# Attention logits of two heads as three half-height products side by side, with undoubled keys and a bias of key sums alone

## The chip, the core and the metric

The kernel runs on one core of one Trainium2 chip. The core has a matrix engine (TensorE, PE in the profile; its weight loads are the row PEld), three engines for elementwise work (VectorE or DVE, ScalarE or ACT, GpSimd or POOL) and SyncE (SP), which here only issues transfers. Matmuls write PSUM, eight banks of 128 partitions by 512 words; GpSimd doesn't read PSUM. The metric is the device time of one execution in microseconds (us), the median of several runs; lower is better.

## The reference

Two layers over 512 tokens of width 1024. Layer 0 is sparse attention: an indexer of 8 heads of width 64 scores every key, each query keeps its best keys, and 16 query heads in 4 groups attend to them. Layer 1 is a "forgetting" attention of 16 heads with a causal mask. Both are followed by an MLP with squared ReLU. What matters here is the logits of each:

```python
idx_logits = einsum('bqhd,bsd->bqhs', qib, ki)           # indexer, d = 64
score = einsum('bqhs,bqh->bqs', relu(idx_logits), wib)   # best keys by this score
logits = einsum('bqngd,bqknd->bqngk', qg, k_sel) * scale # attention A, then softmax

log_f = log_sigmoid(f_logit + b_f)                       # attention B: forget gates
cum = cumsum(log_f)
logits = einsum('bqhd,bshd->bhqs', qb, k) * scale
decay = cum[t, h] - cum[s, h]
logits = where(causal, logits + decay, -inf)             # then softmax
```

Everything is in float32. A softmax over the keys s doesn't change when a number that depends on the query t alone is added to its row.

## The kernel before

**Precision.** A float32 matmul is made of matmuls in fp32r, a reduced format. `split` (line 499) makes a high part (ACT writes the rounded copy) and a low part (DVE subtracts it from the source). A full product is then three matmuls, `mm3` (line 534): high by high, high by low, low by high.

**Logits.** A head has width 64, half of the array's 128 rows. Before, the two halves of the rows are used together for one head. `unpair` (line 681) writes for each of two heads a stationary tile with the high part of the query in 64 rows and its low part in the other 64: two ACT operations and two DVE operations, each on 64 partitions. The keys stand twice, in both halves of the rows, once as high and once as low parts. Two matmuls of 128 rows then give all four products of high and low parts:

```python
for i in range(2):
    PE.matmul(b[:, :n], q[:, 128 * t:128 * t + 128], ks[e][:, i, :n], start=i == 0, stop=i == 1)
```

This form stands in three places: `scores` (line 742, the indexer, 8 heads, query blocks 1 to 3), attention A (lines 848 to 905, 4 key heads of 4 query heads, query blocks 0 to 3) and `attn` (line 1433, attention B, 8 pairs of heads, query blocks 0 to 3). A query block is 128 queries; block t sees n = 128(t + 1) keys, so the matmuls have 128, 256, 384 or 512 columns.

In A and in the indexer the keys are doubled when they are transposed (`dup_T`). In B, `kproj` (line 1400) computes the keys of two heads in one bank (24 matmuls) and then writes four tiles' worth from it: four ACT copies and four DVE subtractions, each on 64 partitions by 512.

**Bias of B.** `bias` (line 1421) makes for each head and each query block a tile of cum[t] - cum[s] on GpSimd, with -1e30 above the diagonal: it fetches the row of cum of a head to all 128 partitions from DRAM (`cd`), and per block runs one tensor_scalar (with the query's own sums, `cq`, as a scalar per partition) and one affine_select on the last 128 columns. `cq` comes from four transposes of `cum` on TensorE. A DVE reduction adds a tile to the logits in the bank and takes the row's minimum of the negated sum; ACT then computes the exponentials, GpSimd scales by the reciprocal sum, TensorE transposes, and the products with the values follow.

**Forget gates.** `fb` (line 1322, 16 matmuls with 48 columns) gives the gate logits; a chain of small DVE operations on 16 partitions (lines 1367 to 1389) gives `cum`, after the value projection in the program's order.

**Order of the work.** The program is recorded and then planned: `Recorder.schedule` (line 244) runs a list schedule over the five engines with estimated costs (`cost`, line 210; a matmul of n columns is max(n/2400 + 0.0133, 0.109) us, whatever its rows). The priority of an operation is the place of the program on TensorE's clock at which it stands, or earlier if its successors need it. A tile is taken only when a slot is free: the logits of A and B may hold three of the eight PSUM banks (`"lg": 3`), the transposes four and the value products one; the indexer's banks have no such limit. The planned order is then emitted; each engine executes its instructions in that order.

**Weights.** Weight tiles are split too. Where a stage's number stands in `far`, the low part is made by ACT (a negated copy) and an accumulating transfer issued by GpSimd, not by DVE.

Line 423 of the profile is the helper that emits every operation, so groups are read by their tiles' names: `lg` and `ix` are banks of logits, `qs`, `qo`, `qst` split queries, `kdup`, `kd`, `kid` doubled keys, `bt` bias tiles, `pT` transposes, `pv` value products, `kp`, `qp` key and query projections, `gc` small transposes of gains.

Of the kernel before, what the change touches and what calls it, by code (L numbers as in the profile page):

```python
# [15 lines left out]
T = 512  # L16
# [4 lines left out]
BIG = 3e38  # L21


class View:
# [35 lines left out]
    def row(self, r):  # L60

        ids = np.broadcast_to(self.ids[:1], (2,) + self.ids.shape[1:])
        return View(self.t, ids, self.chain + [("f", lambda ap: bass.AP(
            tensor=ap.tensor, offset=ap[r:r + 1].offset, ap=[[0, 128], [1, ap.shape[1]]]))])

# [60 lines left out]
class Recorder:  # L126
# [22 lines left out]
    def add(self, eng, fn, a, k):  # L149
# [3 lines left out]
        outs = [k["out"]] if "out" in k else [a[0]]  # L153
        ins = [x for x in list(a[0 if "out" in k else 1:]) + [v for q, v in k.items() if q not in ("out", "accum_out")]
               if isinstance(x, View)]
# [3 lines left out]
        if fn == "matmul" and not k.get("start"):  # L159
            ins = ins + outs  # L160
# [10 lines left out]
        if fn == "matmul" and k.get("start"):  # L171
            for p in set(outs[0].t.last.values()):
                op.preds[p] = 1
# [238 lines left out]
    def emit(self, order):  # L412
        def real(x):
            if not isinstance(x, View):
                return x
            t = x.t
            if t.real is None:
                t.real = t.store.real.tile(list(t.shape), t.dt, tag="%s%d" % (t.store.tag, t.at[0]), name=t.name)
            return x.real()
        for o in order:  # L420
            a = [real(x) for x in o.a]
            k = {q: real(v) for q, v in o.k.items()}
            getattr(self.engs[o.eng], o.fn)(*a, **k)  # L423
# [11 lines left out]
    "pace": 1.0, "pvb": (4,), "rcb": True, "bord": (0, 1, 2, 3),  # L435
# [3 lines left out]
def body(ctx, tc, a, out):  # L439
# [241 lines left out]
    def unpair(dst, b, scale):  # L681

        up, dn = slice(0, 64), slice(64, 128)
        if CFG["swap"]:
            hi, lo = scr([128, 512], "nh", F32R), scr([128, 512], "nl", F32R)
            b = b.flat() if len(b.shape) > 2 else b
            split(hi, lo, b, scale=scale)
            d = dst if len(dst.shape) == 3 else View(dst.t, dst.ids.reshape(dst.ids.shape[0], 2, -1),
                                                     dst.chain + [("r", "p e a b -> p e (a b)", {})])
            SP.dma_start(f32(d)[up, 0], f32(hi)[up])  # L690
            SP.dma_start(f32(d)[dn, 0], f32(lo)[up])
            SP.dma_start(f32(d)[dn, 1], f32(hi)[dn])
            SP.dma_start(f32(d)[up, 1], f32(lo)[dn])
            return
        S.activation(dst[up, 0], b[up], AF.Copy, scale=scale)
        S.activation(dst[dn, 1], b[dn], AF.Copy, scale=scale)
        V.scalar_tensor_tensor(dst[dn, 0], b[up], scale, f32(dst[up, 0]), op0=OP.mult, op1=OP.subtract)
        V.scalar_tensor_tensor(dst[up, 1], b[dn], scale, f32(dst[dn, 1]), op0=OP.mult, op1=OP.subtract)
# [149 lines left out]
    for t in range(NT):  # L848
# [3 lines left out]
        for kv in range(4):  # L852
# [3 lines left out]
            for h in range(4):  # L856
                b = bank([128, 512], "lg")
                for p in range(2):
                    PE.matmul(b[:, :n], qs[t][kv // 2][:, h % 2, 2 * (kv % 2) + h // 2, :], kd[kv][:, p, :n],
                              start=p == 0, stop=p == 1)  # L860
# [437 lines left out]
    def qstack(p, b):  # L1298
        unpair(qo[p], b, 0.125)
# [11 lines left out]
    for p in range(4, 8):  # L1311
        b = bank([128, T], "qp")
        featprod(xq, wS(wq, 128 * p), b)
        qstack(p, b)

# [7 lines left out]
    for k in range(8):  # L1323
        for i in range(2):
            PE.matmul(fb[0:48], wf[:, k, :], xk[i][k // 2][:, k % 2, :], start=k + i == 0, stop=k + i == 8)

# [40 lines left out]
    z, f2 = scr([16, T], "z"), scr([16, T], "f2")  # L1367
    S.copy(f2, fb[32:48])
    V.scalar_tensor_tensor(z, fb[0:16], bfc, f2, op0=OP.add, op1=OP.add)
    e = scr([16, T], "e")  # L1370
    V.tensor_scalar(e, z, -1.0, None, op0=OP.mult)
    V.tensor_tensor(e, z, e, op=OP.min)
    S.activation(e, e, AF.Exp)
    V.tensor_scalar(z, z, 0.0, None, op0=OP.min)
    s = scr([16, T], "s")
    V.tensor_scalar(s, e, 2.0, None, op0=OP.add)
    V.reciprocal(s, s)
    V.tensor_tensor(s, s, e, op=OP.mult)
    w2 = scr([16, T], "w2")
    V.tensor_tensor(w2, s, s, op=OP.mult)  # L1380
    V.tensor_scalar(e, w2, 2.0 / 17, 2.0 / 15, op0=OP.mult, op1=OP.add)
    for c in (13, 11, 9, 7, 5, 3, 1):
        V.tensor_tensor(e, e, w2, op=OP.mult)
        V.tensor_scalar(e, e, 2.0 / c, None, op0=OP.add)
    V.tensor_tensor(e, e, s, op=OP.mult)
    V.tensor_tensor(z, z, e, op=OP.subtract)
    cum, zrow = scr([16, T], "cum"), scr([16, T], "zrow")
    V.memset(zrow, 0.0)
    V.tensor_tensor_scan(cum, z, zrow, 0.0, op0=OP.add, op1=OP.add)
    cd = rec.tile(p_dr["cd"], [16, T], F32, "cd")  # L1390
    SP.dma_start(cd, cum)
    cq = const([128, NT, 16], "cq")
    cb = bank([128, NT, 16], "cb")
    for t in range(NT):
        PE.transpose(cb[:, t, :], cum[:, 128 * t:128 * t + 128], ident[0:16, 0:16])
    S.copy(cq, cb)

    lows("k")

    def kproj(p):  # L1400
# [3 lines left out]
        ks = [htile([128, 2, T], "kdup", F32R) for _ in range(2)]  # L1404
        if CFG["dup"]:

            kn = htile([128, 2, T], "kn", F32R)
            split(kn[:, 0, :], kn[:, 1, :], b)
            for e in range(2):
                for o in range(2):  # L1410
                    SP.dma_start(f32(ks[e])[64 * o:64 * o + 64], f32(kn)[64 * e:64 * e + 64])
            return ks
        for e in range(2):
            r, o = slice(64 * e, 64 * e + 64), slice(64 - 64 * e, 128 - 64 * e)
            S.copy(ks[e][r, 0, :], b[r])
            S.copy(ks[e][o, 0, :], b[r])
            V.tensor_tensor(ks[e][r, 1, :], b[r], f32(ks[e][r, 0, :]), op=OP.subtract)
            V.tensor_tensor(ks[e][o, 1, :], b[r], f32(ks[e][r, 0, :]), op=OP.subtract)
        return ks

    def bias(p):
        bt = [rec.tile(p_bt, [128, 2, 128 * (t + 1)], F32, "bt") for t in range(NT)]
        for e in range(2):
            ck = scr([128, T], "ck")
            SP.dma_start(ck, cd.row(2 * p + e))
            for t in range(NT):
                n = 128 * (t + 1)
                G.tensor_scalar(bt[t][:, e, :], ck[:, :n], -1.0, cq[:, t, 2 * p + e:2 * p + e + 1], op0=OP.mult, op1=OP.add)
                dg = bt[t][:, e, n - 128:n]
                G.affine_select(dg, dg, pattern=[[-1, 128]], compare_op=OP.is_ge, fill=NEG, base=0, channel_multiplier=1)  # L1430
        return [[x[:, e, :] for x in bt] for e in range(2)]

    def attn(p, ks, bts):
        pts = {}
        for e in range(2):
            q = qo[p][:, e, :]
            b0, b1, b2 = [bank([128, T], "pT") for _ in range(3)]
            rcs = small(4, "rc") if CFG["rcb"] else None
            sts = small(4, "st") if CFG["rcb"] else None
            ls = {}  # L1440
            l01 = scr([128, 384], "l")
            for t in CFG["bord"]:
                n = 128 * (t + 1)
                b = bank([128, 512], "lg")
                for i in range(2):
                    PE.matmul(b[:, :n], q[:, 128 * t:128 * t + 128], ks[e][:, i, :n], start=i == 0, stop=i == 1)
                l, mn = scr([128, n], "l") if t > 1 else l01[:, 128 * t:128 * t + n], small(1, "mn")
                st = sts[:, t:t + 1] if CFG["rcb"] else small(1, "st")
                V.tensor_tensor_reduce(out=l, in0=b[:, :n], in1=bts[e][t], op0=OP.add, op1=OP.min,
                                       scale=-1.0, scalar=BIG, accum_out=mn)  # L1450
                S.activation(l, l, AF.Exp, bias=mn, scale=-1.0, accum_out=st)
                ls[t] = l, st
            if CFG["rcb"]:
                V.reciprocal(rcs, sts)
            for t in CFG["bord"]:
                l, st = ls[t]
                if CFG["rcb"]:
                    rc = rcs[:, t:t + 1]
                else:
                    rc = small(1, "rc")  # L1460
                    V.reciprocal(rc, st)
# [47 lines left out]
    bts = {0: bias(0)}  # L1509
# [78 lines left out]
```

## Time and profile before

| | us |
|---|---|
| median of three runs (lowest, highest) | 1147.61 (1146.72, 1148.46) |
| the profiled execution | 1144.4 |
| its span, first to last instruction | 1142.6 |
| indexer's products | about 34 to 56 of the span |
| attention A | about 106 to 204 |
| MLP of layer 0 | about 204 to 555 |
| queries, gates and values of B | about 555 to 650 |
| attention B with its key projections | about 650 to 776 |
| output projection and MLP of layer 1 | about 776 to 1142 |

A row of the profile gives an operation's engine, the tile that it writes and those that it reads, its shape, its count, and busy time and mean duration. For matmuls, `rows*columns` of the weights stands ahead of the shape. Durations of matmuls overlap, so their pace is read from one start to the next. "issue" as the releaser of an idle time means that the engine waited for nothing that the profile shows.

### The profile page before, as it was taken

How to read it: one execution, taken by the hardware profiler on the slowest of the kernel's cores; microseconds unless marked ns; L12 is line 12 of the kernel's file. 1: busy time of each engine (PE TensorE's matmuls, PEld its weight loads, DVE VectorE, ACT ScalarE, POOL GpSimd, SP SyncE). 2: the span in 40 equal slices, each digit the busy share in tenths (PEclk: the TensorE clock that was granted, in tenths of full speed). 3: DMA queues.
4: the chain of work that ended last, by engine and by line, in shares of the span. 5: the costliest groups of instructions: out<-in, count | busy, mean ns of one | idle time of the engine just before them, and what ended most of it. 6: DMA issues, size and time to landing. Idle time of an engine off the chain costs nothing. (4 is left out here: it accounts for less than half of the span.)

```text
span 1142.6 us, 18657 instructions
## 1 busy us (share of the span) xinstructions
PE 1118.7 (98%) x6671; PEld 975.2 (85%) x6671; DVE 975.9 (85%) x1709; ACT 818.5 (72%) x1432; POOL 225.1 (20%) x376
## 2 busy tenths in 40 slices
PE   8999999999999999999999999999999999999997
PEld 8877778899899898898897787788998998998985
DVE  7999997488988979979898979783789889799687
ACT  8942899677666667579787369997676666666693
POOL 0212455100010100101101068872000100001040
PEclk9999999999999999999999999999999999999999
DMA  9871262836674674795577443579356755847892
GB/s 339 179 166 37 77 183 44 196 91 187 185 183 150 166 203 148 166 274 157 138 237 184 85 129 108 171 184 213 82 185 169 180 167 166 221 144 191 234 219 79
DMA packets 117708, 189.04 MB, mean 165 GB/s; under 512 B 8136, under 2 KB 63456, under 8 KB 117616
## 3 DMA queue, kind: packets, MB, share of 16 engines
q1 hardware_dynamic: 102640, 133.33, 35.3%
q0 software_dynamic: 14976, 54.53, 26.2%
q8 instruction: 52, 0.85, 0.3%
q14 instruction: 40, 0.33, 0.1%
HBM read 129.09 MB, written 4.23 MB: 117 GB/s over the span
## 5 line engine op out<-in xcount | busy, mean ns | idle before, releaser
L423 PE MATMUL tp<-dhi,xhi 128*128 128x512 f32 (+1 forms) x484 | 183.3, 389 | 2.8 <-DVE h L423 1.6
L423 PE MATMUL tp<-dlo,xhi 128*128 128x512 f32 (+1 forms) x484 | 183.3, 388 | 0.0
L423 PE MATMUL tp<-dhi,xlo 128*128 128x512 f32 (+1 forms) x484 | 182.3, 388 | 0.0
L423 ACT CAST dhi<-raw 128x1024 fp32r<-128x1024 f32 x126 | 129.4, 1048 | 72.0 <-DVE raw L423 55.0
L423 PE MATMUL up<-t,uhi 128*128 128x256 f32 x896 | 148.8, 284 | 2.4 <-DVE r L423 2.3
L423 DVE TENSOR_TENSOR dlo<-raw,dhi 128x1024 fp32r<-128x1024 f32 x108 | 130.4, 1217 | 15.6 <-ACT dhi L423 9.2
L423 POOL DMA_DIRECT2D ulo<-raw x42 | 36.7, 873 | 514.5 <-ACT ulo L423 421.1
L423 PEld LDWEIGHTS up<-t,uhi 128*128 128x128 f32 x896 | 126.6, 192 | 4.0 <-DVE r L423 3.4
L423 DVE TENSOR_TENSOR raw<-raw 128x1024 f32<-128x1024 f32 x100 | 120.2, 1216 | 0.4
L423 PE MATMUL up<-xT,uhi 128*128 128x256 f32 x672 | 117.2, 284 | 0.2 <-DVE r L423 0.2
L423 PEld LDWEIGHTS tp<-dhi,xhi 128*128 128x128 f32 x484 | 90.9, 188 | 22.7 <-ACT hg L423 2.0
L423 PEld LDWEIGHTS tp<-dhi,xlo 128*128 128x128 f32 x484 | 90.8, 188 | 18.3
L423 PEld LDWEIGHTS tp<-dlo,xhi 128*128 128x128 f32 x484 | 90.9, 188 | 17.9
L423 PEld LDWEIGHTS up<-xT,uhi 128*128 128x128 f32 x672 | 99.1, 191 | 2.7 <-DVE r L423 1.8
L423 PE MATMUL up<-t,ulo 128*128 128x256 f32 x448 | 96.0, 283 | 0.0
L423 ACT CAST uhi<-raw 128x1024 fp32r<-128x1024 f32 x84 | 86.0, 1044 | 4.8 <-PE up L423 4.7
L423 PE MATMUL tp<-whi,xT 128*128 128x512 f32 (+2 forms) x304 | 88.2, 366 | 0.6 <-ACT xT L423 0.5
L423 DVE TENSOR_TENSOR h<-tp,h 128x512 f32<-128x512 f32 (+1 forms) x97 | 64.8, 677 | 26.4 <-PE tp L423 26.3
L423 PE MATMUL up<-xT,ulo 128*128 128x256 f32 x336 | 80.7, 283 | 0.0
L423 POOL TENSOR_SCALAR l<-l,rc 128x128 f32<-128x128 f32 (+3 forms) x128 | 70.1, 565 | 49.0 <-DVE rc L423 32.4
L423 ACT ACTIVATE l<-l,mn 128x128 f32<-128x128 f32 (+3 forms) x128 | 71.4, 561 | 6.4 <-DVE mn L423 6.0
L423 PEld LDWEIGHTS up<-t,ulo 128*128 128x128 f32 x448 | 72.4, 192 | 0.0
(233 smaller groups left out, 2689.6 us busy)
## 6 DMA issues: line engine op xcount, KB each, us to landing
raw<-in_w_down_dram SPq DMA_DIRECT2D x96, 512.0 KB, 5.5
raw<-in_w_up_dram SPq DMA_DIRECT2D x64, 512.0 KB, 5.8
wlo<-raw POOLq DMA_DIRECT2D x44, 512.0 KB, 6.8
ulo<-raw POOLq DMA_DIRECT2D x42, 512.0 KB, 5.6
raw<-in_w_kv_b_dram SPq DMA_DIRECT2D x22, 512.0 KB, 5.6
dlo<-raw POOLq DMA_DIRECT2D x18, 512.0 KB, 6.0
raw<-in_w_in_a_dram SPq DMA_DIRECT2D x12, 512.0 KB, 8.3
raw<-in_w_o_a_dram SPq DMA_DIRECT2D x8, 512.0 KB, 5.7
```

Source lines behind the costliest of these rows:

```text
L423: getattr(self.engs[o.eng], o.fn)(*a, **k)
```

## The change

- `logits` takes two heads at once. The queries of two heads lie on the two halves of the rows, as high and low parts in tiles of their own, and so do the keys. Three products, high by high, high by low and low by high, are each a "twin": two matmuls of 64 rows, one for each head, emitted one right after the other, into two banks. The planner takes a twin as one operation with the cost of one matmul, and it needs both banks at once. Two heads thus take 6 matmuls of 64 rows where they took 4 of 128. The low by low product is no longer computed.
- `unpair` goes. Queries are split with one ACT and one DVE operation on 128 partitions.
- `kproj` splits the keys of two heads once: one ACT and one DVE operation where there were four and four. In A and the indexer the keys stay doubled, and each head uses its own half of them.
- The bias is -cum[s] alone. `z` gets the other sign before the scan. For two heads two tiles are fetched, of 256 and 512 columns, and the diagonal is masked in them. The tile of 256 serves query blocks 1 and then 0, that of 512 blocks 3 and then 2: after the DVE reduction of block t = 1 or 3, GpSimd masks the diagonal of block t - 1 in the same tile. The query blocks run in the order 1, 3, 0, 2. `cq`, its transposes and the GpSimd tensor_scalar operations go.
- In `attn` the logits and exponentials of both heads now come first, then the scaling and transposes of one head and of the other.
- The gate's matmuls and its DVE chain stand after the first four query products, ahead of the last four and of the values; the first bias tiles are fetched there.
- `far` takes in the value products 1 and 2.

```diff
+    def rows(self, r, m):
+        ids = np.broadcast_to(self.ids[:1, None], (2, m) + self.ids.shape[1:])
+        return View(self.t, ids, self.chain + [("f", lambda ap: bass.AP(
+            tensor=ap.tensor, offset=ap[r:r + 1].offset, ap=[[0, 128], [T, m], [1, ap.shape[1]]]))])
...
+            if o.fn == "twin":
+                for i in (0, 3):
+                    self.engs[o.eng].matmul(*a[i:i + 3], **k)
+                continue
...
-    "far": ("v3", "v7", "v4"),
+    "far": ("v1", "v2", "v3", "v7", "v4"),
...
-    "pace": 1.0, "pvb": (4,), "rcb": True, "bord": (0, 1, 2, 3),
+    "pace": 1.0, "pvb": (4,), "rcb": True, "bord": (1, 3, 0, 2),
...
+    def logits(bs, q, k):
+        for i, (x, y) in enumerate(((0, 0), (0, 1), (1, 0))):
+            a = []
+            for e, b in enumerate(bs):
+                r = slice(64 * e, 64 * e + 64)
+                a += [b, q[x][r], k[y][r]]
+            PE.twin(*a, start=i == 0, stop=i == 2)
...
-        unpair(dst, b, scale)
+        split(dst[:, 0], dst[:, 1], b, scale=scale)
...
-            b = bank([128, 512], "ix")
-            for p in range(2):
-                PE.matmul(b[:, :n], qst[t][:, h % 2, h // 2, :], kid[:, p, :n], start=p == 0, stop=p == 1)
+            if h % 2 == 0:
+                bs = [bank([128, 512], "ix") for _ in range(2)]
+                logits([b[:, :n] for b in bs], [qst[t][:, i, h // 2, :] for i in range(2)], [kid[:, i, :n] for i in range(2)])
+            b = bs[h % 2]
...
-    V.tensor_tensor(z, z, e, op=OP.subtract)
+    V.tensor_tensor(z, e, z, op=OP.subtract)
...
+    def diagonal(x, j):
+        dg = x[:, 128 * j:128 * j + 128]
+        G.affine_select(dg, dg, pattern=[[-1, 128]], compare_op=OP.is_ge, fill=NEG, base=0, channel_multiplier=1)
+
+    def bias(p):
+        bt = []
+        for n in (256, 512):
+            x = rec.tile(p_bt, [128, 2, n], F32, "bt")
+            SP.dma_start(x, cd[:, 0:n].rows(2 * p, 2))
+            bt.append([x[:, e, :] for e in range(2)])
+            for e in range(2):
+                diagonal(bt[-1][e], n // 128 - 1)
+        return bt
...
-        ks = [htile([128, 2, T], "kdup", F32R) for _ in range(2)]
...
+        ks = htile([128, 2, T], "kn", F32R)
+        split(ks[:, 0, :], ks[:, 1, :], b)
...
+        for t in CFG["bord"]:
+            n = 128 * (t + 1)
+            bs = [bank([128, 512], "lg") for _ in range(2)]
+            logits([b[:, :n] for b in bs], [qo[p][:, i, 128 * t:128 * t + 128] for i in range(2)],
+                   [ks[:, i, :n] for i in range(2)])
+            for e in range(2):
+                l, mn = scr([128, n], "l") if t > 1 else l01[e][:, 128 * t:128 * t + n], small(1, "mn")
+                V.tensor_tensor_reduce(out=l, in0=bs[e][:, :n], in1=bts[t // 2][e][:, :n], op0=OP.add, op1=OP.min,
+                                       scale=-1.0, scalar=BIG, accum_out=mn)
+                if t % 2:
+                    diagonal(bts[t // 2][e], t - 1)
+                S.activation(l, l, AF.Exp, bias=mn, scale=-1.0, accum_out=sts[e][:, t:t + 1])
```

More of the change, by code (lines that the diff above doesn't have):

```diff
@@ L152, in add @@
         op.prio, op.preds, op.succ, op.tiles, op.new = op.seq + self.off, {}, [], [], []
-        outs = [k["out"]] if "out" in k else [a[0]]
+        outs = [k["out"]] if "out" in k else [a[0], a[3]] if fn == "twin" else [a[0]]
         ins = [x for x in list(a[0 if "out" in k else 1:]) + [v for q, v in k.items() if q not in ("out", "accum_out")]
-               if isinstance(x, View)]
+               if isinstance(x, View) and (fn != "twin" or x is not a[3])]
         if k.get("accum_out") is not None:
@@ L158, in add @@
         outs = [x for x in outs if isinstance(x, View)]
-        if fn == "matmul" and not k.get("start"):
+        if fn in ("matmul", "twin") and not k.get("start"):
             ins = ins + outs
@@ L170, in add @@
                 t.reads.setdefault(c, []).append(op)
-        if fn == "matmul" and k.get("start"):
-            for p in set(outs[0].t.last.values()):
-                op.preds[p] = 1
+        if fn in ("matmul", "twin") and k.get("start"):
+            for v in outs:
+                for p in set(v.t.last.values()):
+                    op.preds[p] = 1
         if fn == "matmul":
@@ L679, in rope @@
             e.tensor_tensor(dst, dst, tmp, op=OP.add)
[L681 to L698, printed above, removed]
+    def logits(bs, q, k):
[5 more added lines that the diff above has]
+            PE.twin(*a, start=i == 0, stop=i == 2)
     def stacks(dst, src, scale):
@@ L856, in body @@
             for h in range(4):
[L857 to L860, printed above, removed]
+                if h % 2 == 0:
+                    bs = [bank([128, 512], "lg") for _ in range(2)]
+                    logits([b[:, :n] for b in bs], [qs[t][kv // 2][:, i, 2 * (kv % 2) + h // 2, :] for i in range(2)],
+                           [kd[kv][:, i, :n] for i in range(2)])
+                b = bs[h % 2]
                 l = scr([128, 512], "l")
@@ L1298, in qstack @@
     def qstack(p, b):
-        unpair(qo[p], b, 0.125)
+        split(qo[p][:, 0, :], qo[p][:, 1, :], b, scale=0.125)
     wq = a["w_q_b"][0]
@@ L1310, in body @@
         qstack(i, bs[i])
[L1311 to L1314, printed above, removed]
     fraw = scr([128, 8, 16], "fraw")
@@ L1325, in body @@
             PE.matmul(fb[0:48], wf[:, k, :], xk[i][k // 2][:, k % 2, :], start=k + i == 0, stop=k + i == 8)
+    z, f2 = scr([16, T], "z"), scr([16, T], "f2")
+    S.copy(f2, fb[32:48])
+    V.scalar_tensor_tensor(z, fb[0:16], bfc, f2, op0=OP.add, op1=OP.add)
+    e = scr([16, T], "e")
+    V.tensor_scalar(e, z, -1.0, None, op0=OP.mult)
+    V.tensor_tensor(e, z, e, op=OP.min)
+    S.activation(e, e, AF.Exp)
+    V.tensor_scalar(z, z, 0.0, None, op0=OP.min)
+    s = scr([16, T], "s")
+    V.tensor_scalar(s, e, 2.0, None, op0=OP.add)
+    V.reciprocal(s, s)
+    V.tensor_tensor(s, s, e, op=OP.mult)
+    w2 = scr([16, T], "w2")
+    V.tensor_tensor(w2, s, s, op=OP.mult)
+    V.tensor_scalar(e, w2, 2.0 / 17, 2.0 / 15, op0=OP.mult, op1=OP.add)
+    for c in (13, 11, 9, 7, 5, 3, 1):
+        V.tensor_tensor(e, e, w2, op=OP.mult)
+        V.tensor_scalar(e, e, 2.0 / c, None, op0=OP.add)
+    V.tensor_tensor(e, e, s, op=OP.mult)
+    V.tensor_tensor(z, e, z, op=OP.subtract)
+    cum, zrow = scr([16, T], "cum"), scr([16, T], "zrow")
+    V.memset(zrow, 0.0)
+    V.tensor_tensor_scan(cum, z, zrow, 0.0, op0=OP.add, op1=OP.add)
+    cd = rec.tile(p_dr["cd"], [16, T], F32, "cd")
+    SP.dma_start(cd, cum)
+    def diagonal(x, j):
[10 more added lines that the diff above has]
+        return bt
+    for p in range(4, 8):
+        b = bank([128, T], "qp")
+        featprod(xq, wS(wq, 128 * p), b)
+        qstack(p, b)
+    bts = {0: bias(0)}
     vb = [[big([128, 8, 2, 64], "vb") for _ in range(2)] for _ in range(NT)]
@@ L1365, in body @@
             tokprod(xl(xk), wkv, 0, 8, D + 512 * n, 512, lambda t, b, n=n: vout(t, n, b))
[L1367 to L1385, printed above, removed]
-    V.tensor_tensor(z, z, e, op=OP.subtract)
[L1387 to L1396, printed above, removed]
     lows("k")
@@ L1403, in kproj @@
         featprod(xk, u, b)
-        ks = [htile([128, 2, T], "kdup", F32R) for _ in range(2)]
[L1405 to L1418, printed above, removed]
@@ L1419, in kproj @@
-        return ks
[L1421 to L1431, printed above, removed]
+        ks = htile([128, 2, T], "kn", F32R)
@@ L1433, in attn @@
+        split(ks[:, 0, :], ks[:, 1, :], b)
+        return ks
     def attn(p, ks, bts):
         pts = {}
+        sts, l01 = [small(4, "st") for _ in range(2)], [scr([128, 384], "l") for _ in range(2)]
+        ls = [{}, {}]
+        for t in CFG["bord"]:
+            n = 128 * (t + 1)
+            bs = [bank([128, 512], "lg") for _ in range(2)]
+            logits([b[:, :n] for b in bs], [qo[p][:, i, 128 * t:128 * t + 128] for i in range(2)],
[7 more added lines that the diff above has]
+                S.activation(l, l, AF.Exp, bias=mn, scale=-1.0, accum_out=sts[e][:, t:t + 1])
+                ls[e][t] = l
@@ L1435, in attn @@
         for e in range(2):
-            q = qo[p][:, e, :]
             b0, b1, b2 = [bank([128, T], "pT") for _ in range(3)]
[L1438 to L1441, printed above, removed]
+            rcs = small(4, "rc")
+            V.reciprocal(rcs, sts[e])
             for t in CFG["bord"]:
[L1443 to L1461, printed above, removed]
+                l, rc = ls[e][t], rcs[:, t:t + 1]
                 if CFG["bsc"] == "V" or (p, e) in CFG["bsv"]:
@@ L1508, in body @@
     kss = {0: kproj(0)}
-    bts = {0: bias(0)}
     for p in range(8):
```

## The prediction

> **What bounds the kernel now.** I read the totals of the page first, then busy time by stretches, cut where the tiles of the logits begin and end.
>
> ```profile
> span 1142.6 us, 18657 instructions
> PE 1118.7 (98%) x6671; PEld 975.2 (85%) x6671; DVE 975.9 (85%) x1709; ACT 818.5 (72%) x1432; POOL 225.1 (20%) x376
> ```
>
> ```profile
> 34.00:56.00 22.00, 21.51 (x113) 17.75 (x112) 20.56 (x51) 21.62 (x41) 2.59 (x3) 1.00 0.77 151
> 106.00:204.00 98.00, 97.33 (x536) 76.06 (x536) 87.09 (x270) 87.22 (x218) 44.98 (x76) 1.00 0.38 97
> 555.00:609.00 54.00, 53.22 (x332) 47.64 (x331) 48.31 (x91) 42.03 (x90) 1.76 (x2) 1.00 0.64 194
> 609.00:650.00 41.00, 40.28 (x175) 31.46 (x174) 37.57 (x51) 26.00 (x35) 5.24 (x6) 1.00 0.60 124
> 650.00:776.00 126.00, 121.89 (x670) 99.75 (x669) 100.64 (x253) 105.11 (x250) 92.23 (x198) 1.00 0.50 139
> ```
>
> The columns are PE, PEld, DVE, ACT, POOL, then the granted clock, the share of DMA and GB/s. The rows are the indexer, attention A, the queries of B, forget gate and values, attention B. TensorE (PE) is busy nearly throughout, at a granted clock of 1.00. The idle that shows in these five stretches is 0.49 + 0.67 + 0.78 + 0.72 + 4.11 = 6.8 us. So DVE and ACT, 80 to 83% busy in attention B, can give back at most these 6.8 us; the rest of the change is worth what it does to TensorE's own time.
>
> Matmuls overlap, so their time is read from start to start, not from their durations. The chain of waits has two long runs, of 512 and of 256 columns, and the timeline one of 128:
>
> ```profile
> 655.72 7.71 PE kp L423 x33
> 895.98 34.53 PE up L423 x286
> ```
>
> ```profile
> 113.35 0.86 PE L423 MATMUL lg<-kd,qs 128*128 128x128 f32 x6
> 114.05 0.68 PE L423 MATMUL tp<-whi,xT 128*128 128x512 f32 x2
> ```
>
> Per matmul that is 7.71/33 = 0.234 us at 512 columns, 34.53/286 = 0.121 at 256, on the line between them 0.177 at 384, and (114.05 - 113.35)/6 = 0.117 at 128, nearly as much as at 256: there the weight load (128 columns wide for each) sets the pace.
>
> **The logits' products.** By tile, the matmuls that write them:
>
> ```profile
> L423 PE MATMUL ix<-kid,qst x48: 276/338/499, 34.9 to 53.9; 128*128 128x256 f32 x16, 128*128 128x384 f32 x16, 128*128 128x512 f32 x16
> L423 PE MATMUL lg<-kd,qs x128: 220/342/523, 109.3 to 186.9; 128*128 128x128 f32 x32, 128*128 128x256 f32 x32, 128*128 128x384 f32 x32, 128*128 128x512 f32 x32
> L423 PE MATMUL lg<-kdup,qo x128: 218/336/478, 663.3 to 760.3; 128*128 128x128 f32 x32, 128*128 128x256 f32 x32, 128*128 128x384 f32 x32, 128*128 128x512 f32 x32
> ```
>
> One matmul of each width is 0.117 + 0.121 + 0.177 + 0.234 = 0.649 us, so A and B cost 32 x 0.649 = 20.8 us each, the indexer 16 x 0.532 = 8.5, together 50 us. Two heads took four full matmuls; they will take three pairs of half-height ones. No row of before shows two half-height matmuls at once. A pair costs between one full matmul (halves side by side) and two (one after the other): 37.5 us or 75 in all, -12.5 or +25. I take -12.5, since the two halves read different rows and write different banks, and nothing they use is shared but the queue. The Trainium skill (TensorE: Matmul & The Clock Gate, Part 3) measures a speedup of 3.07 for four quarter-height matmuls side by side and puts their starts about 4 ns apart; by it a pair also costs about one matmul. No run here shows that yet.
>
> **What it costs to change the array's division.** This is the term that decides. Before has a few matmuls that use part of the rows: gains are transposed with 8 rows in the midst of a dense stretch, the decay with 16.
>
> ```profile
> 235.64 0.39 PE L423 MATMUL tp<-whi,oT 128*128 128x512 f32 x1
> 235.96 0.22 PE L423 MATMUL gc<-ident,gqr 8*128 8x8 f32 x1
> 236.05 0.20 PE L423 MATMUL gc<-ident,gkvr 8*128 8x8 f32 x1
> 236.18 0.50 PE L423 MATMUL up<-xT,whi 128*128 128x256 f32 x2
> 236.52 0.28 PE L423 MATMUL up<-xT,wlo 128*128 128x256 f32 x1
> ```
>
> ```profile
> 235.96 0.13 PEld L423 LDWEIGHTS gc<-ident,gqr 8*128 8x128 f32 x1 [0.35 <-issue]
> ```
>
> ```profile
> 118.94 0.19 PEld L423 LDWEIGHTS pv<-pf,vf 128*64 128x64 f32 x2 [0.33 <-issue]
> ```
>
> The load of the first small transpose stands idle for 0.35 us with no semaphore to blame, and a load of a 64-column matmul in A stands idle for 0.33 in the same way. From 235.64 to 236.52 are 0.88 us. The 512-column matmul (0.234) and the two of 256 (0.241) account for 0.475; 0.405 is left for two tiny matmuls, the way in and the way out. The tiny ones cost between nothing and 0.09 each (235.96 to 236.05), so one excursion costs 0.22 to 0.41 us. I take the middle, 0.31. The Trainium skill (TensorEngine Tiling, Tiling Modes) says that changing the tiling mode, not just the tile, drains TensorE. It speaks against this change, and these rows agree with it at 8 rows and at 64 columns; 64 rows were not used.
>
> How many excursions? A group is the three pairs of one query block and one pair of heads. A and B have 8 x 4 each, 64 in all. A group takes two of the three banks that the logits may hold, so the next group waits until one of them is read, and the planner, for which a pair costs no more than one matmul, fills that time with full matmuls: each group is an excursion of its own. The indexer has all eight banks and ran its products in long runs; I give its 12 groups 6 excursions. A group can also be torn:
>
> ```profile
> 705.54 0.36 PE L423 MATMUL lg<-kdup,qo 128*128 128x256 f32 x1
> 705.74 0.50 PE L423 MATMUL pT<-ident,l 128*128 128x128 f32 x3
> 706.00 0.36 PE L423 MATMUL lg<-kdup,qo 128*128 128x256 f32 x1
> ```
>
> Here transposes stand between the two products of one bank. I take 70 excursions, at most 85. 70 x 0.31 = 21.7 us; the ends are 64 x 0.22 = 14.1 and 85 x 0.405 = 34.4.
>
> **Splits of queries and keys.** Row by row, half-height work costs as much as full-height:
>
> ```profile
> L423 DVE TENSOR_TENSOR kdup<-kp,kdup 64x512 fp32r<-64x512 f32 x32 | 22.0, 688 | 9.5 <-ACT kdup L423 9.0
> L423 ACT CAST kdup<-kp 64x512 fp32r<-64x512 f32 x32 | 18.6, 581 | 8.8 <-PE kp L423 4.4 <-DVE kdup L423 4.0
> L423 DVE TENSOR_TENSOR pl<-pT,ph 128x512 fp32r<-128x512 f32 x42 | 27.2, 683 | 2.7 <-ACT ph L423 2.6
> L423 DVE SCALAR_TENSOR_TENSOR qs<-qT,qs 64x512 fp32r<-64x512 f32 x16 | 11.0, 689 | 0.4
> L423 DVE SCALAR_TENSOR_TENSOR qo<-qp,qo 64x512 fp32r<-64x512 f32 x16 | 11.0, 689 | 0.3
> L423 ACT ACTIVATE qo<-qp 64x512 fp32r<-64x512 f32 x16 | 9.6, 598 | 3.8 <-PE qp L423 3.6
> ```
>
> A full-height subtraction takes 0.683, a half-height one 0.688. Of 32 key operations on each engine 8 remain: DVE loses 24 x 0.688 = 16.5 us, ACT 24 x 0.581 = 13.9, all in attention B. For qo DVE loses 8 x 0.689 = 5.5 and ACT 8 x 0.598 = 4.8, for qs DVE 5.5 again. That lies beside TensorE; what it can bring is the idle of 6.8 us, of which I take half, -3.4, because part of that idle is start-up of single matmuls and waits on POOL and transfers.
>
> **Bias tiles, gate, order.** By tile:
>
> ```profile
> L423 POOL TENSOR_SCALAR bt<-ck,cq x64: 362/582/1548, 660.8 to 754.6; 128x512 f32<-128x512 f32 x16, 128x384 f32<-128x384 f32 x16, 128x256 f32<-128x256 f32 x16, 128x128 f32<-128x128 f32 x16
> L423 POOL TENSOR_SCALAR_AFFINE_SELECT bt<-bt x64: 282/292/603, 667.0 to 761.3; 128x128 f32<-128x128 f32 x64
> ```
>
> POOL loses the 64 tensor_scalars, 64 x 0.582 = 37 us of its 92 in attention B; the 64 selects stay. POOL isn't the bound: nothing for the sum. The keys' sums now arrive as two tiles for two heads, 256 + 512 columns for each head where one row of 512 was fetched: half as much again, at a DMA share of 0.50, hidden. Half of the selects now wait for the DVE reduction of block 1 or 3 and must end before that of block 0 or 2. Behind such a reduction on DVE stands the rest of the softmax; exposed in full that would be 32 x 0.292 = 9.3 us of DVE, less than the 16.5 it loses, so nothing reaches TensorE. The bank rule above is the other new wait: TensorE is in order, so a pair whose banks are unread holds up all behind it. With single banks that wait was small:
>
> ```profile
> PE pv L423 <- DVE mn L423: 0.6, 1, 0.6
> ```
>
> I leave it at nothing, because other matmuls are planned ahead, and let it eat the other half of the idle. The gate's chain of small DVE operations goes ahead of four query products and the values; PE runs 33 key products the moment it ends (655.72), so earlier sums change the order and hardly the end: nothing. The four transposes of the sums go too, with their excursion: counted in the rounding. Values 1 and 2 move four low parts to DMA:
>
> ```profile
> L423 DVE TENSOR_TENSOR dlo<-raw,dhi 128x1024 fp32r<-128x1024 f32 x108 | 130.4, 1217 | 15.6 <-ACT dhi L423 9.2 <-DMA ulo<-raw 5.4 <-PE up L423 0.5
> L423 ACT ACTIVATE dlo<-dhi 128x1024 fp32r<-128x1024 f32 x18 | 18.7, 1058 | 0.0
> ```
>
> DVE loses 4 x 1.217 = 4.9 us, ACT gains 4 x 1.058 = 4.2 and POOL four issues, where ACT was busy 26 of 41 us: covered. Without that cover, the accumulating transfer would hold up the first value product, once.
>
> **The sum.** The profiled execution took 1144.4 us (span 1142.6), 3.2 under the median of 1147.6. 1144.4 - 12.5 + 21.7 - 3.4 = 1150.2, and 3.2 more against the median: 1153.4.
>
> **Rivals.** (1) The division changes for nothing at 64 rows, or the stall falls into waits: 1144.4 - 12.5 - 3.4 + 3.2 = 1131.7, with the idle at its ends 1128 to 1135. For it speaks that not every use of part of the array stalls:
>
> ```profile
> 608.52 0.39 PE L423 MATMUL qp<-xT,wlo 128*128 128x512 f32 x1
> 608.74 3.86 PE L423 MATMUL fb<-xT,wf 128*48 128x512 f32 x16
> 612.44 0.40 PE L423 MATMUL tp<-dhi,xT 128*128 128x512 f32 x1
> ```
>
> Sixteen 48-column matmuls take 3.70 us, 0.231 each, with no gap on the way in (0.22) or out. Against it: that one keeps all 128 rows, and the 8-row one stalled. By the page on tiling this rival should not occur. (2) The two weight loads of a pair go one after the other. Then no pair is shorter than 2 x 0.117 = 0.234 us: three pairs of four widths cost 2.80 us for two heads against 2.59 now, +3.3 us over 16 pairs of heads, the indexer about as now, and 3.2 + 21.7 - 3.4 = +21.5 gives 1169.1. It decides wherever a pair has under 512 columns. (3) The halves don't run at once at all, so the change doesn't do what it says: +25 + 21.7 - 3.4 gives 1190.9, without stalls 1169.2. (4) Groups run together, or half of the stalls lie in waits: 35 x 0.31 = 10.9, so -12.5 + 10.9 - 3.4 = -5.0 gives 1142.6.
>
> **How the numbers follow.** Forecast 0.42 (own range 1146 to 1163: excursions and their price between the ends), rival 1 0.30, rival 2 0.13, rival 3 0.05, rival 4 0.10. A measurement can tell about 0.2% from no change, 2.3 us. Faster by more: 0.30 + 0.08 of rival 4 = 0.38. Within: 0.07 of the forecast and 0.02 of rival 4 = 0.09. Slower: 0.35 + 0.13 + 0.05 = 0.53. The range leaves out the lower third of rival 1 and, above, rival 3 and the far part of rival 2: 1130 to 1172.
>
> **What would show it.** In the profile after, pairs of 64-row matmuls whose starts lie a few ns apart, and three of them at 512 columns in some 0.70 us; a gap of 0.1 us or more on each side of a group, weight loads idle "<-issue" some 70 times; DVE some 32 us less busy, POOL 37, and PE's shown idle in attention B under 4.1 us. I am wrong if the load of a group's first half is issued while the full matmul before it still runs (rival 1), if the pairs' starts lie 0.1 us apart (rival 2) or a whole matmul apart (rival 3).

## The result and the profile after

The changed kernel takes 1157.81 us (median of four runs, 1156.18 to 1159.46), the kernel before 1147.16 in the same runs: a ratio of 1.0102, 95% interval 1.0087 to 1.0118: slower by 1.0%, clear of noise. The profiled execution took 1158.42 us, 0.6 over its median; that of the kernel before was 2.8 under (1144.4). First its page:

```profile
span 1156.6 us, 18774 instructions
PE 1140.7 (99%) x6819; PEld 966.3 (84%) x6819; DVE 941.6 (81%) x1662; ACT 799.7 (69%) x1392; POOL 198.0 (17%) x316
```

The span is 14.0 us longer, where the medians are 10.6 us apart; the profiles thus show some 3 us more than the change costs. DVE has 34 us less to do, ACT 19, POOL 27; TensorE is busy 22 us longer. Where the 14 us lie is read from the first start (the fourth pair of numbers) of three tiles that mark the stages: the first MLP, the queries of B, the keys of B. Before:

```profile
L423 PE MATMUL up<-xT,whi x256: 278/283/384, 236.2 to 835.9; 128*128 128x256 f32 x128
L423 PE MATMUL qp<-xT,whi x192: 278/283/397, 555.2 to 608.3; 128*128 128x256 f32 x128, 128*128 128x512 f32 x64
L423 PE MATMUL kp<-xT,whi x128: 387/393/500, 646.4 to 747.9; 128*128 128x512 f32 x128
```

After:

```profile
L435 PE MATMUL up<-xT,whi x256: 278/283/384, 246.8 to 850.6; 128*128 128x256 f32 x128
L435 PE MATMUL qp<-xT,whi x192: 278/283/404, 565.0 to 621.8; 128*128 128x256 f32 x128, 128*128 128x512 f32 x64
L435 PE MATMUL kp<-xT,whi x128: 389/395/686, 656.2 to 762.6; 128*128 128x512 f32 x128
```

Up to the first `up` product (the output projection of attention A lies ahead of it), where only the logits and the query splits differ, 10.6 us are lost (246.8 - 236.2). From there to the queries of B 0.8 are won, from the queries to the keys nothing changes (91.2 us both times), and from the keys to the end 4.2 are lost (500.4 for 496.2). So attention A with the indexer loses most, and it has no new bias, no moved gate and no other value products.

A stretch of attention B shows what happens on TensorE, first a group that another matmul tears apart, then a whole one:

```profile
670.26 0.39 PE L435 MATMUL kp<-xT,wlo 128*128 128x512 f32 x1
670.57 0.50 PE L433 MATMUL lg<-kn,qo 64*128 64x256 f32 x4
671.01 0.50 PE L435 MATMUL kp<-xT,whi 128*128 128x512 f32 x1
671.43 0.39 PE L433 MATMUL lg<-kn,qo 64*128 64x256 f32 x2
671.75 0.49 PE L435 MATMUL kp<-xT,whi 128*128 128x512 f32 x1
672.08 0.39 PE L435 MATMUL kp<-xT,wlo 128*128 128x512 f32 x1
672.31 0.40 PE L435 MATMUL kp<-xT,whi 128*128 128x512 f32 x1
672.64 0.96 PE L433 MATMUL lg<-kn,qo 64*128 64x512 f32 x6
673.53 0.50 PE L435 MATMUL kp<-xT,whi 128*128 128x512 f32 x1
673.87 0.39 PE L435 MATMUL kp<-xT,wlo 128*128 128x512 f32 x1
```

and the weight loads of the whole group:

```profile
672.64 0.53 PEld L433 LDWEIGHTS lg<-kn,qo 64*128 64x128 f32 x6 [0.36 <-issue]
673.53 0.19 PEld L435 LDWEIGHTS kp<-xT,whi 128*128 128x128 f32 x1 [0.36 <-issue]
```

Six half-height matmuls of 512 columns stand between 672.64 and 673.53, 0.89 us with the way out. At a full matmul's pace of 0.234 one after the other would be 1.40; three pairs are 0.70. The halves run side by side. But here the loads stand idle 0.36 us on the way in and again on the way out, with no semaphore to blame. From 672.31 to 673.87 are 1.56 us for two full matmuls and three pairs, 5 x 0.234 = 1.17 at their pace: the excursion costs 0.39. The torn group pays twice: 1.82 us from 670.26 to 672.08 for three full matmuls (0.70) and three pairs of 256 columns (0.36), so 0.76 for two excursions.

**An account of TensorE's time.** I gave each matmul of a trace its pace (0.227 us at 512 columns, 0.120 at 256, in proportion to the columns between and at least 0.109; a half-height one half of that; a transpose 0.109) and summed what is left of the time from its start to the next. Then I split these gaps: those from the matmul ahead of an unbroken run of logits to the second one behind it, and all others.

| | matmuls at pace, us | runs of logits | gaps around them, us | other gaps, us |
|---|---|---|---|---|
| before (full height) | 1090.9 | 118 | 7.6 | 36.3 |
| after (half height) | 1078.5 | 115 | 43.0 | 27.3 |

So -12.4 from the products, +35.4 around the runs, -9.0 elsewhere: the 14.0 us of the two spans. An excursion costs 43.0/115 = 0.37 us, where full-height runs had 0.06. The single amounts depend on the paces by some us, the differences less: with the paces of the prediction the runs lose 36.0 in place of 35.4.

The starts also show of what an excursion is made. Against the prediction's paces (a pair like one full matmul), the medians over the traces of after, e1 and e8 are 0.09 us lost ahead of the first pair, 0.10 between the first pair and the second, 0.09 ahead of the first full matmul behind the run, and 0.10 between that and the next. From the second pair on the pairs of a run follow one another at the pace of full matmuls, to 4 ns in the median, also in runs of twelve matmuls and more.

### The profile page after: what moved, and what is told of

Its sections match the earlier page's. It is cut to its first block, busy times and chain, and to the rows that moved or that the text cites. A ratio compares the mean times of both kernels' runs of the same rounds, so it can differ in the third digit from the quotient of the medians.

```text
span 1156.6 us, 18774 instructions
## 1 busy us (share of the span) xinstructions
PE 1140.7 (99%) x6819; PEld 966.3 (84%) x6819; DVE 941.6 (81%) x1662; ACT 799.7 (69%) x1392; POOL 198.0 (17%) x316
## 4 chain that ended last, share of the span: by engine, by line
PE 67%; DVE 6%; ACT 2%; issue 1%; DMA 1%; DVEq 0%; ACTq 0%
PE tp L435 31%; PE up L435 25%; PE kp L435 4%; PE lg L433 2%; PE pv L435 2%; PE pT L435 2%; DVE xlo L435 1%; DVE raw L435 1%; DMA ulo<-raw 1%; DVE e L435 1%; DVE h L435 1%; ACT xT L435 1%; DVE s L435 1%; PE yT L435 1%; PE qp L435 0%
## 5 line engine op out<-in xcount | busy, mean ns | idle before, releaser
L435 DVE TENSOR_TENSOR dlo<-raw,dhi 128x1024 fp32r<-128x1024 f32 x104 | 125.5, 1216 | 14.7 <-ACT dhi L435 9.2
L435 POOL TENSOR_SCALAR l<-l,rc 128x384 f32<-128x384 f32 (+3 forms) x128 | 69.0, 565 | 74.4 <-DVE rc L435 50.5
```

## The experiments

The theory: the products gain what was meant, and the changes of the array's division, 115 times 0.37 us, take it three times over, because the planner tears groups and knows no price for it. Rivals: waits on the banks, taken two at a time; and the rest of the change (bias, gate, value products). All ratios are to the kernel before on the same chip in the same runs. That kernel took 1146.4 us beside e1 to e4, 1146.3 beside e5 to e8 and 1145.5 beside e9 to e12, so from one of these sets to another the ratios are compared (0.001 is 1.15 us). The count of runs is that of the planned order, and the traces show the same counts.

**e1: groups kept whole.** The three pairs are one operation for the planner, and its six matmuls are emitted together.

```diff
-            PE.twin(*a, start=i == 0, stop=i == 2)
+        PE.trio(*a, start=True)
```

> The changed kernel, but the three pairs of a group are one operation for the planner, so nothing comes between them. The planned order then has 71 runs of half-height matmuls where the changed kernel has 115; the products themselves and their pace are the same. Theory (each run costs about 0.37 us for changing the array's division there and back): 44 runs fewer, 16 us less than the changed kernel's 1157.8, about 1142, not above 1148 if a third of it is lost again in waits. Rival 1 (two banks out of three make TensorE wait for DVE's reads): the banks are as before, so within 2 us of 1157.8. Rival 2 (the new bias tiles, the earlier gate or the value products cost the time): within 2 us of 1157.8.

Measured: 1143.96 us, ratio 0.9979 (0.9964 to 0.9995). 13.9 us less than the changed kernel, with the same arithmetic, the same banks and the same rest. Its page:

```profile
span 1143.6 us, 18746 instructions
PE 1125.2 (98%) x6819; PEld 963.0 (84%) x6819; DVE 942.0 (82%) x1662; ACT 799.0 (70%) x1392; POOL 197.0 (17%) x316
```

The other engines' work is that of the changed kernel to 1 us; TensorE's row is 15.5 us shorter. By the ratios it is 14 us for 44 runs, 0.32 each: the gaps around runs fall by 16.4 us, others rise by 3.4. Of the list of waits one row of each kernel, after and e1:

```profile
PEld lg L433 <- issue: 16.2, 64, 0.4
```

```profile
PEld lg L434 <- issue: 8.0, 27, 0.4
```

The loads of logits that wait for nothing the profile shows fall from 64 times to 27. Both rivals fall as the main cause: neither the number of banks nor the rest was touched.

**e2: the logits undone, the rest kept.** Two full-height products for each head, doubled keys and queries (the removed lines put back).

> The changed kernel with the logits undone: two full-height products for each head, queries and keys doubled as before; new bias tiles, gate, order of the blocks and value products stay. No half-height matmul is left. Theory: the products cost 12 us more, the runs' 43 us are gone, and what DVE and ACT had given back is lost: the kernel before or a little under it, 1140 to 1148. Rival 1 (banks; they are still taken two at a time here for the reductions, but each product needs one): 1147 to 1150. Rival 2 (the rest costs the time): 1155 or more.

Measured: 1154.2 us, 1.0067 (1.0041 to 1.0093). The theory did not have this. Rival 2's 1155 lies within the interval, so by its total alone this run speaks for rival 2; what speaks against it is where the time is lost. In the part up to the first MLP nothing is lost against the kernel before (first `up` at 235.8 for 236.2), as the theory says. But attention B loses, and so do the values. The rows that mark the stages, and the first two of TensorE's waits:

```profile
L435 PE MATMUL qp<-xT,whi x192: 274/283/397, 554.2 to 611.0; 128*128 128x256 f32 x128, 128*128 128x512 f32 x64
L435 PE MATMUL kp<-xT,whi x128: 387/390/687, 649.5 to 755.7; 128*128 128x512 f32 x128
```

```profile
PE pT L435 <- POOL l L435: 4.6, 4, 2.4
PE tp L435 <- ACT m L435: 2.6, 1, 2.6
```

From queries to keys are 95.3 us where before and after have 91.2, and TensorE waits for an ACT copy of the values and for GpSimd's scaling ahead of the transposes. So the rest of the change isn't free: with the full-height logits and the old splits it costs some 8 us.

**e3: the logits alone.** The half-height logits, single keys and full-height splits; bias, gate, order of blocks and value products as before. The logits of the two heads of attention B still come first together, as in the changed kernel.

> The kernel before with the logits' part of the change alone: half-height pairs, queries and keys split once; bias tiles from the queries' and the keys' sums, gate, order of the blocks and value products as before. The planned order has 104 runs of half-height matmuls. Theory: 11 runs fewer than in the changed kernel, 4 us less, and nothing else of weight: 1151 to 1159. Rival 2 (the rest costs the time): 1147 or less.

Measured: 1164.68 us, 1.0156 (1.0135 to 1.0177), slower than the whole change, above what I had expected. The account gives 42.1 us of gaps around 104 runs and 35.4 elsewhere. So the loss is here without the rest, and is larger: the rest of the change gives back some 6 us by the ratios when it stands with half-height logits. Other gaps fall from 35.4 to 27.3.

**e4: four banks for the logits.** e1 with `"lg": 4`.

> As e1_whole, with four banks for the logits instead of three, so that a second group can be computed before the first is read. 66 runs planned. Theory: 5 runs fewer than e1_whole, 2 us less than that. Rival 1 (banks): this is where the time comes back, 5 us or more under e1_whole. Rival 2: as e1_whole.

Measured: 1140.53 us, 0.9949 (0.9935 to 0.9964), 3.4 us less than e1. Five runs fewer are 1.9 us at 0.37; at most 1.5 is left for the banks. They matter little.

**e5 and e6: what in the rest cost e2 its time.** e5 puts the two heads of attention B one after the other again:

```diff
-        for t in CFG["bord"]:
...
-            bs = [bank([128, 512], "lg") for _ in range(2)]
...
+        for e in range(2):
+            for t in CFG["bord"]:
...
+                b = bank([128, 512], "lg")
```

> e2_old_logits with the two heads of attention B one after the other again: a head's four blocks of logits, then its scaling and transposes, then the other head. Bias tiles, gate and value products stay new. Theory A (with full-height products the joint order of two heads delays the first transposes, which cost e2 some 5 us in attention B): 1154.2 - 5 = 1149, with the stretch from the first key projection to the second MLP back at the 166 us of the kernel before. Theory B (the earlier gate and the value products cost it): no change, within 2 us of 1154.2.

e6 puts the gate's chain behind the values and the low parts of value products 1 and 2 on DVE:

```diff
-    "far": ("v1", "v2", "v3", "v7", "v4"),
+    "far": ("v3", "v7", "v4"),
```

> e2_old_logits with the gate's chain behind the values again and value products 1 and 2 with their low parts on DVE again; bias tiles and the joint order of two heads stay new. Theory B (with the half-height splits of queries still on ACT and DVE, the earlier gate and the ACT work of the value products cost e2 some 4 us between the first query product and the first key product): 1154.2 - 4 = 1150, that stretch back at 91 us. Theory A: within 2 us of 1154.2.

Measured: e5 1147.82 us, 1.0021 (1.0008 to 1.0033); e6 1144.44 us, 0.9987 (0.9976 to 0.9999). Each was expected to exclude the other, and each alone takes back most of the 8 us or all of it (5.3 and 9.2 by the ratios). Of e5:

```profile
L435 PE MATMUL qp<-xT,whi x192: 274/283/398, 554.7 to 611.5; 128*128 128x256 f32 x128, 128*128 128x512 f32 x64
L435 PE MATMUL kp<-xT,whi x128: 387/389/498, 650.2 to 750.8; 128*128 128x512 f32 x128
```

From queries to keys it still has the 95.5 us of e2, but from the first key product to the end (of its span of 1144.7 us) 494.5, where e2 has 500.3: what theory A says. The stretch that e6 was to mend is mended, 647.1 - 555.9 = 91.2:

```profile
L435 PE MATMUL qp<-xT,whi x192: 274/283/397, 555.9 to 608.9; 128*128 128x256 f32 x128, 128*128 128x512 f32 x64
L435 PE MATMUL kp<-xT,whi x128: 387/393/500, 647.1 to 748.1; 128*128 128x512 f32 x128
```

but e6 also gains in attention B (495.5 us from the first key product to the end), which theory B did not say. So with full-height products the loss in attention B needs both the joint order of the heads and the earlier gate with its value products; without either one it is gone. e6, with full-height products, new bias and both heads together, is about as fast as the kernel before, so there these cost nothing together.

**e9: the late gate in the changed kernel.** As e6, with the half-height logits.

> The changed kernel with the gate's chain behind the values again and value products 1 and 2 with their low parts on DVE again; half-height logits, splits and bias tiles stay. 113 runs are planned. Theory (the runs of half-height matmuls make the loss, the earlier gate costs only where ACT and DVE still carry the old splits): within 4 us of 1157.8. Theory B (the earlier gate and the value products cost 10 us everywhere, as they did in e2): 1148 or so.

Measured: 1154.67 us, 1.0088 (1.0073 to 1.0103); the changed kernel had 1.0102 (1.0087 to 1.0118). The early gate with its value products costs the change some 2 us by the ratios, within the intervals, not 10. Beside e3 this run shows more: the two kernels differ in the bias tiles and the order of the blocks alone, and e9 is 0.0068 under it, 8 us. So with half-height logits the new bias and order are worth 8 us, where with full-height ones (e6) they were worth next to nothing.

**e10: e3 with groups kept whole.**

> e3_only_logits (1164.7) with each group kept whole for the planner, as e1_whole is to the changed kernel. 70 runs are planned for 104. Theory (0.32 us for a run, from the changed kernel and e1_whole): 34 fewer, 11 us, 1154; the new bias tiles, gate and order then still give 10 us to e1_whole. Rival (what e3 loses lies in waits on the old bias, not in runs): 1160 or more.

Measured: 1151.73 us, 1.0060 (1.0043 to 1.0077). By the ratios 11 us for 34 runs, 0.32 each, as from the changed kernel to e1: the same price in other surroundings. The distance to e1, 9 us, is again what the rest gives when it stands beside half-height logits.

**e7 and e8: fewer runs still.** e7 computes together what fits into two banks (four heads of blocks 0 and 1 in A, blocks 1 and 0 in B; in the indexer four heads at a time, over four banks where two don't hold them), e8 the wide blocks too, over four banks; both with four banks for the logits and the blocks of B in the order 1, 0, 3, 2. In both (and in e11 and e12) the planner also counts 0.3 us for a run, which it did not in e1 and e4. The edit of attention B in e8, shortened (`several` makes the groups one run, here of twelve matmuls):

```diff
-            bs = [bank([128, 512], "lg") for _ in range(2)]
-            logits([b[:, :n] for b in bs], ...
+            if t not in got:
+                ts = next(x for x in ((1, 0), (3, 2)) if t in x)
+                got.update(zip(ts, several("lg", [(128 * (u + 1), ...
+            bs = got[t]
```

> Groups put together where they fit in banks: in attention A four heads of blocks 0 and 1 in two banks, in B blocks 1 and 0 in two banks, in the indexer four heads at a time; the rest one group each; four banks for the logits, blocks of B in the order 1, 0, 3, 2. 50 runs of half-height matmuls are planned where e4_whole_lg4 has 66; all products are the same. Theory (a run costs 0.3 to 0.4 us): 16 runs fewer, 5 to 6 us less than the 1140.5 of e4, 1135. Rival 1 (banks: a bank is held until two blocks are read): 1140 or more.

> As e7_pack2, and two groups of the wide blocks are put together over four banks too, in A and in B. 35 runs are planned. Theory: 31 runs fewer than e4_whole_lg4, 9 to 12 us less, 1129 to 1132. Rival 1 (banks: a run now needs all four banks that the logits may hold, so the next one waits for eight reads by DVE or ACT): no better than e7_pack2, 1135 to 1145.

Measured: e7 1137.45 us, 0.9927 (0.9911 to 0.9943); e8 1133.25 us, 0.9892 (0.9873 to 0.9910). Each run removed still pays, but less than expected: by the ratios e7 is 2.5 us under e4 where 5 to 6 were expected, e8 6.5 where 9 to 12 were. The page of e8:

```profile
span 1128.7 us, 18723 instructions
PE 1112.2 (99%) x6819; PEld 962.5 (85%) x6819; DVE 939.2 (83%) x1662; ACT 795.4 (70%) x1392; POOL 196.5 (17%) x316
```

TensorE does the same 6819 matmuls as in the changed kernel in 28.5 us less. The account over the five kernels that have the same bias, gate and value products (matmuls at pace 1078.5 us in all):

| | runs | gaps around them, us | for one run | other gaps, us | ratio |
|---|---|---|---|---|---|
| after | 115 | 43.0 | 0.37 | 27.3 | 1.0102 |
| e1 | 71 | 26.6 | 0.37 | 30.7 | 0.9979 |
| e4 | 66 | 25.3 | 0.38 | 30.1 | 0.9949 |
| e7 | 50 | 20.8 | 0.42 | 28.3 | 0.9927 |
| e8 | 35 | 14.0 | 0.40 | 28.4 | 0.9892 |

The gaps around a run stay at 0.37 to 0.42 us, and their number decides. In time a run less gives 0.32 us from after to e1, 0.16 from e4 to e7 and 0.27 from e7 to e8, by the ratios. The rows are those of the profiled executions, and that of e4 was its slowest, 2.9 us over the median.

**e11: six banks for e8.**

> e8_pack4 with six banks for the logits instead of four: 34 runs are planned for 35. Theory (runs): within 2 us of 1133.3. Rival 1 (banks: a run of four banks waits for eight reads): 4 us or more under it.

Measured: 1131.31 us, 0.9887 (0.9872 to 0.9902), e8 within the intervals. Banks are not what is left. This and e8 are the fastest versions, 1.1% under the kernel before; e1, e4 and e7 are under it too, by 0.2, 0.5 and 0.7%.

**e12: the late gate in e8.**

> e8_pack4 with the gate's chain and the value products as in the kernel before. 35 runs are planned. Theory: within 3 us of 1133.3; where TensorE has less to do the later gate may cost a few us at the start of attention B, or give back what ACT is spared in the values.

Measured: 1144.0 us, 0.9989 (0.9973 to 1.0004), 10.8 us above e8, 11 by the ratios: far outside. Two stretches of attention B, by windows, of e12 and then of e8:

```profile
740.00:760.00 20.00, 17.94 (x103) 13.06 (x102) 10.98 (x34) 15.74 (x34) 8.43 (x17) 1.00 1.03 247
760.00:780.00 20.00, 16.48 (x91) 11.20 (x89) 10.08 (x32) 11.58 (x32) 7.96 (x17) 1.00 0.34 92
```

```profile
740.00:760.00 20.00, 20.00 (x117) 15.94 (x116) 10.31 (x29) 19.90 (x39) 9.46 (x17) 1.00 0.78 171
760.00:780.00 20.00, 20.00 (x108) 16.48 (x107) 10.10 (x23) 11.11 (x22) 6.23 (x12) 1.00 0.79 188
```

The first figure behind the length is TensorE's: 17.94 and 16.48 of 20 us where e8 has 20.00. The key products and the logits of B show a difference, again e12 and then e8:

```profile
L443 PE MATMUL kp<-xT,wlo x64: 387/394/497, 640.1 to 720.8; 128*128 128x512 f32 x64
L436 PE MATMUL lg<-kn,qo x192: 217/335/497, 654.0 to 774.0; 64*128 64x256 f32 x48, 64*128 64x128 f32 x48, 64*128 64x512 f32 x48, 64*128 64x384 f32 x48
```

```profile
L443 PE MATMUL kp<-xT,wlo x64: 387/397/497, 641.1 to 733.4; 128*128 128x512 f32 x64
L436 PE MATMUL lg<-kn,qo x192: 217/335/501, 654.8 to 760.7; 64*128 64x256 f32 x48, 64*128 64x128 f32 x48, 64*128 64x512 f32 x48, 64*128 64x384 f32 x48
```

In e12 the last key product starts 53 us ahead of the last logits, in e8 27. The last pairs of heads of e12 thus have no key products among them. The same distance is 57 and 54 us in e3 and e10, whose attention B is 7 and 9 us longer than that of e9 and e1, and 12 to 24 in all other kernels. So attention B is long where the key products are used up early; that this is the cause is not shown, since which matmuls the planner keeps to fill attention B was not varied by itself. The place of the gate, moved together with the value products, is worth 9 us to e6 in one direction, 11 to e8 in the other and little to the changed kernel. Why it turns is not settled.

## Why the prediction came out as it did

The way was right, the size was half of it: +5.8 us forecast, +10.6 measured, inside the range. In part that is luck: the excursions cost some 14 us more than forecast, and 6 us more than forecast came back elsewhere, for the most part from edits that were put at nothing. By its steps:

- **TensorE bounds the kernel.** Right: DVE lost 34 us (forecast 32), and the kernel is slower. On DVE and ACT half-height work costs as much as full-height, as the rows of the new splits show (8 in place of 32, at the same duration):

```profile
L435 DVE TENSOR_TENSOR kn<-kp,kn 128x512 fp32r<-128x512 f32 x8 | 5.5, 688 | 6.4 <-ACT kn L435 6.4
L435 ACT CAST kn<-kp 128x512 fp32r<-128x512 f32 x8 | 4.7, 588 | 6.2 <-PE kp L435 6.1
```

- **Products, -12.5.** Right: -12.4, if a half-height matmul is given half the time of a full one. That this fits the pairs show: inside a run they follow one another like full matmuls (to 4 ns in the median), and the two matmuls of a pair start 12 ns apart at most, their two loads 9, over all 228 pairs. This was a choice between two ends, and that disposes of rivals 2 and 3.
- **The price of an excursion, 0.31 out of 0.22 to 0.41.** Right in kind, some 0.06 low: 0.37 over 115 runs. The row that led there, two tiny transposes of 8 rows, was a good stand-in, though its own work had to be bounded; the upper end was nearer. The Trainium skill (TensorEngine Tiling, Tiling Modes) says that a change of mode drains TensorE, and at 64 rows this trace agrees: some 0.19 us are lost on the way in and again on the way out. Rival 1 is out. Its sign was badly chosen: the load at 672.64 does start before the end that the profile gives the full matmul ahead (672.31 + 0.40), because durations overlap; the starts decide, not the ends.
- **The number of excursions, 70, at most 85.** This is the term that was mis-sized: 115. I had seen that a group can be torn and quoted an instance, and then allowed for few. A group of three pairs has two places to be torn where one of two products had one, and the indexer, given 6 runs, shows 14. In A and B the runs are 101, not 64; the loads of logits that wait for "issue" are 64, near the 70 of the forecast, but they are not all of the runs. Number and price together are 43.0 us where the sum had 21.7; against the 7.6 that lay around full-height runs it is +35.4.
- **What the other engines give back, -3.4 of 6.8.** In all other gaps fell by 9.0, but little of that came from the splits: e3, which has them without the rest, has 35.4 us of other gaps, 0.9 under before. The bound of 6.8 was no bound. It was taken from the idle that the windows show, but a matmul's duration in the profile (0.39 us at 512 columns) is longer than its pace (0.23), so gaps of up to 0.16 us count as busy. After the change attention B shows TensorE busy for all of its 141 us, although gaps stand in it:

```profile
655.00:796.00 141.00, 141.00 (x773) 103.31 (x773) 84.12 (x227) 103.91 (x238) 63.85 (x131) 1.00 0.57 150
```

- **Bias, gate and value products, nothing.** Wrong for the bias: with half-height logits the bias tiles and the order of the blocks give 8 us (e3 and e9), and the whole rest 6 to 9 (e3 and after, e10 and e1). The gate with the value products is nearly nothing here (e9, some 2 us), but e2 and e12 show that the rest costs 8 us, and the early gate gives 11, in other surroundings. Which wait of the old bias costs the 8 us stays open. POOL lost 27 us, not 37: its issues for the value products and slower selects took part of it back.
- **Waits on the banks, nothing.** About right: loads of logits wait for the reductions (`mn`) for 3.6 us in all, before 1.3, and a fourth bank gives at most 1.5 (e4). The row that the prediction shows for it is one of value products, not of logits.
- **Rival 4, groups run together,** is what e8 makes true with 35 runs: below the kernel before by 1.1%.

So the lost time is explained by the theory, in number and price: e1 and e10 change only how the products are grouped, and the time follows the number of runs. What of the rest helps or hurts beside which logits is shown for the bias with the order of the blocks, and for the gate with the value products, not for each alone.

## What to carry to other kernels

Half-height matmuls side by side paid for themselves here only in long runs: a run must save more than the 0.37 us of its gaps, and three pairs in place of four full matmuls save 0.12 to 0.23. So count the changes of the array's division, not the matmuls, and give a planner the whole run as one operation before asking it to fill gaps. Where an engine is dense, measure its slack from start to start; the idle that a profile shows is only what durations don't cover.

## What the runs showed of the hardware

The gaps around a run hardly depend on its length: 0.37 us with six matmuls or fewer in nearly all runs (after), 0.40 with twelve or more (e8). They stand at the changes: 0.09 us ahead of the first matmul behind a change of the array's division and 0.10 ahead of the second, on the way in and on the way out; behind that, pairs of half-height matmuls keep the pace of full ones. The two weight loads of a pair run as closely together as the matmuls: six loads of 128 columns took 0.41 us with a duration of 0.18 each, in a group of 128 columns:

```profile
675.35 0.41 PEld L433 LDWEIGHTS lg<-kn,qo 64*128 64x128 f32 x6 [0.37 <-PE kp L435]
```
